# The first FFN of a decoder trunk, from eight block products to seven

## The chip, the core and the metric

One core of a Trainium2 chip runs the whole program in one launch. The metric is the time of one execution on the device in microseconds (us); the core has a matrix engine (PE, with a part PEld that loads weights), a vector engine (DVE), an activation engine (ACT), a general engine (POOL), and a queue engine (SP) that here only issues transfers. POOL issues transfers too, those that add to what lies in their target.

## What is computed

A trunk of two layers on one sequence of 512 tokens, model width 1024, all in float32. Each layer is: a half-step SwiGLU FFN (hidden width 2816), a token mixer, and another half-step FFN. The mixer of the first layer is a short gated convolution, that of the second a sparse attention. So there are six sub-layers, here numbered s = 0 to 5: FFN, convolution, FFN, FFN, attention, FFN. Each of them does

```python
h = rms_norm(x, g) * (1 + scale) + shift          # adaLN
x = x + HALF * gate * ((silu(h @ w_g) * (h @ w_u)) @ w_out)   # an FFN
```

with shift, scale and gate (1024 numbers each) from the conditioning vector c: `mod = silu(c) @ ada_w + ada_b`. That is a product of one row with a 1024 x 18432 matrix for the two layers: each of its 144 pieces of 128 outputs is done on DVE, as a row sum over a 128 x 1024 tile that is read from memory (512 KB), not on PE. The text calls such a piece a **modulation tile**; sub-layer s has 24 of them (8 scale, 8 shift, 8 gate).

## The kernel before

The state x lies in SBUF as eight tiles of 128 channels x 512 tokens. Every float32 product is made of three products of rounded parts (`mm3`, L167 to L170): high by high, high by low, low by high, so each operand is kept as a high part and a low part. A weight tile comes in by `weights` (L172): SP issues the load into `wraw`, ACT copies it to `whi`, DVE subtracts to get `wlo` (`split`, L163). `wraw`, `whi` and `wlo` have three buffers each in the pool `wp`.

**The usual FFN** (`ffn`, L462; s = 2, 3 and 5). The 22 hidden blocks j of 128 columns each need a gate product g and an up product u. The first two j are done plainly while the normalised input is still coming (`head_start`, L342, tile `hs`), the third as a `pair` (L407), each half of the tokens for itself; a plain j is 2 x 8 x 3 = 48 products of 512 columns, or twice as many of 256. Then `quarters` (L314) forms four sums of the quarters of h (tiles `th`, `tl`), and the remaining 19 j go by `seven_products` (L471): the 2 x 2 block product that makes g and u for two halves of the depth and two halves of the tokens takes seven block products of 4 x 3 matmuls each at 256 columns, so 84, and sums of weight quarters beside it. For these SP loads two quarters into the tile `qa`, POOL issues a transfer that adds a third quarter to both (L488), SP loads the whole block into `wraw` and a quarter into `a22`; DVE adds (L492, L493) and everything is split into high and low parts. `qa` has four places in turn: two of a pool `swa`, and two (`hhi1`, `hlo1`) that the second token half of h leaves when the third j is done (L477 to L479). The sums of the products are DVE's (L521 to L527). The output product runs in four parts of the hidden blocks (`FOUR` = 6, 6, 6, 4): after a part, for each of eight output blocks d, one weight tile, 3 x 6 matmuls of 512 columns into `y`, and an addition to x on DVE (L557). The last part goes in token halves, so that the next norm can begin.

**The first FFN** (`ffn_first`, L419; s = 0) is another function: all 22 j plain, three of them in its head (L433), with the modulation tiles of s = 0 between them (`ada_first`, L142); three output parts of 8, 7 and 7. It loads weights through further buffers of the pool `ap` (argument `own`), which also has four buffers for modulation tiles.

**The order of the modulation tiles.** They are jobs in a list (`todo`, L1192); `spread` (L370) hands a few to each step of a stage. The code gives the first FFN the 16 of its head, 8 gate tiles, all 24 of s = 1 and 12 of s = 2; the convolution (`conv`, L595) gets the other 84. A framework orders the instructions of every engine when the kernel is built, by their place in the program and by when operands and buffers are free, so a job may run earlier than its place. At run time each engine, SP's queue too, works in its built order. A small table for the attention's bias (`bias_table`, L649, eight matmul instructions in plain float32) is made in the first FFN by the job `small` (L1200).

PSUM has eight banks; six of them serve the products in turn (`psum`, L71), two the norm and the attention.

Of the kernel before, what the change touches and what calls it, by code (L numbers as in the profile page):

```python
# [12 lines left out]
F32 = mybir.dt.float32  # L13
# [15 lines left out]
PARTS = ((0, 8), (8, 15), (15, 22))  # L29
# [23 lines left out]
def decoder_kernel(ctx, tc, xT, cT, ng, adaw, adab, ffi, ffo, cwi, cw, cwo,  # L53
# [30 lines left out]
    ap = ada_es.enter_context(tc.tile_pool(name="ada", bufs=4))  # L84
    cond = ap.tile([P, D], F32, name="cond", bufs=1)
    x = [cst.tile([P, T], F32, name=f"x{d}") for d in range(KD)]
    ngs = cst.tile([P, NSUB * KD], F32, name="ngs")
    adabs = cst.tile([P, NSUB * NMOD], F32, name="adabs")
    for d in range(KD):
        (nc.sync if d < KD - 2 else nc.gpsimd).dma_start(x[d], xT[d])  # L90
    nc.sync.dma_start(cond, bass.AP(tensor=cT.tensor, offset=cT.offset, ap=[[0, P], [1, D]]))
    nc.gpsimd.dma_start(ngs, ng)
    nc.gpsimd.dma_start(adabs, adab)
    one = ap.tile([P, 1], F32, name="one", bufs=1)
# [12 lines left out]
    nc.scalar.activation(cond, cond, AF.Silu)  # L107
# [7 lines left out]
    def ada_tile(ap, s, t):  # L115
        raw = ap.tile([P, D], F32, name="adaraw")
        nc.sync.dma_start(raw, adaw[s * NADA + t])
        m = mods[:, s * NMOD + t:s * NMOD + t + 1]
        nc.vector.tensor_tensor_reduce(out=raw, in0=raw, in1=cond, scale=1.0, scalar=0.0,  # L119
                                       op0=ALU.mult, op1=ALU.add, accum_out=m)  # L120
# [12 lines left out]
    def ada_gate(s):  # L133
        c = s * NMOD + 2 * KD
        if s % 3 == 1:
            nc.vector.tensor_add(mods[:, c:c + KD], mods[:, c:c + KD], adabs[:, c:c + KD])
        else:
            nc.vector.tensor_add(mods[:, c:c + KD], mods[:, c:c + KD], adabs[:, c:c + KD])
            nc.vector.tensor_scalar(mods[:, c:c + KD], mods[:, c:c + KD], 0.5, None, op0=ALU.mult)


    def ada_first(ap, d):  # L142
        n = 1 if d < 2 else 2
        if d % n == 0:
            for c in range(d, d + n):
                ada_tile(ap, 0, c)
                ada_tile(ap, 0, KD + c)
            ada_scale(0, d, d + n)
            ada_shift(0, d, d + n)

    def ada_jobs(ap, s):
        lo = 2 * KD if s == 0 else 0
        jobs = [(lambda t=t: ada_tile(ap, s, t)) for t in range(lo, NADA)]

        def end():
            if s:
                ada_scale(s, 0, KD)
                ada_shift(s, 0, KD)
            ada_gate(s)
        return jobs + [end]  # L160
# [22 lines left out]

    def project(o, w, wc, h, ks, first, last, a=0, b=T):
        c = slice(wc * P, (wc + 1) * P)
        for n, (kw, k) in enumerate(ks):
            mm3(o, w[0][:, kw, c], w[1][:, kw, c], h[0][k][:, a:b], h[1][k][:, a:b],
                first and n == 0, last and n == len(ks) - 1)
# [29 lines left out]
    class Norm:  # L218
# [62 lines left out]
        def whole(self, d):  # L281
            sc, sh = mod(self.s, 0, d), mod(self.s, 1, d)
            xr = tmp("xr")
            nc.vector.scalar_tensor_tensor(xr, x[d], sc, self.all, op0=ALU.mult, op1=ALU.mult)
            nc.scalar.activation(self.hi[d], xr, AF.Identity, bias=sh)
            nc.vector.scalar_tensor_tensor(self.lo[d], xr, sh, self.hi[d], op0=ALU.add, op1=ALU.subtract)
# [8 lines left out]
        def alloc_seven(self, hp, tf, tt):  # L295
# [6 lines left out]
            self.th = [tt.tile([P, KD // 2, HT], F32R, name=f"th{j}") for j in range(4)]  # L302
            self.tl = [tt.tile([P, KD // 2, HT], F32R, name=f"tl{j}") for j in range(4)]
# [10 lines left out]
        def quarters(self):  # L314
# [92 lines left out]
    def pair(f, j, h, own=None, halves=False):  # L407
        gu = []
        for c in range(2):
            w = ffn_in(f, j, c, own if c else None)  # L410
            o = psum("gu")
            for a, b in HALVES if halves else ((0, T),):
                project(o[:, a:b], w, 0, h, [(k, k) for k in range(KD)], True, True, a, b)
# [5 lines left out]
    def ffn_first(s, f, nrm, nxt, extra, ahead, first, soon, own):  # L419
        with ExitStack() as es:  # L420
            hp = pool(es, "hp", 1)
            hid = Hidden(es, 18)
            h = nrm.alloc(hp)
            nj = FIRST
            early = spread(soon, PARTS[0][1] - nj)
            late = spread(extra, NJ - PARTS[0][1] + 2 * KD)

            def fill():
                early() if soon else late()

            js = [(j, c) for j in range(nj) for c in range(2)]
            w, os = [], [psum("hs") for _ in js]
            for d in range(KD):  # L433
                first(d)
                if d < len(js):
                    w.append(ffn_in(f, *js[d], own=own if d > 2 else None))
                nrm.whole(d)
                for n in range(len(w)):
                    for k in range(0 if n == d else d, d + 1):
                        project(os[n], w[n], 0, h, [(k, k)], k == 0, k == KD - 1)  # L440
            for j in range(nj):
                hid.activate(os[2 * j], os[2 * j + 1])
            for p, (j0, j1) in enumerate(PARTS):
                for j in range(max(j0, nj), j1):
                    hid.activate(*pair(f, j, h, own))
                    fill()
                n = j1 - j0
                a, ka = (hid.hi[j0:j1], hid.lo[j0:j1]), [(k, k) for k in range(n)]
                last = p == len(PARTS) - 1
                for d in range(KD - 3 if last else KD):  # L450
                    w = ffn_out(f, d, 1, j0, j1, own if d % 2 else None)
                    o = psum("y")
                    project(o, w, 0, a, ka, True, True)
                    if last:
                        residual(s, d, o, nxt)
                    else:
                        fill()
                        nc.vector.scalar_tensor_tensor(x[d], o, mod(s, 2, d), x[d], op0=ALU.mult, op1=ALU.add)
            assert not extra
            return tail(s, nxt, [(d, ffn_out(f, d, 1, j0, j1, own), 0, ka) for d in range(KD - 3, KD)], a, ahead)  # L460

    def ffn(s, f, nrm, nxt, w0, ahead):  # L462
        with ExitStack() as es:
# [3 lines left out]
            nj = 2  # L467
# [3 lines left out]
            def seven_products(j):  # L471
# [60 lines left out]
            swa = pool(es, "swa", 1, side="right")  # L532
            with ExitStack() as tf_es:
                nrm.alloc_seven(hp, pool(tf_es, "tf", 1), tt)
                h = nrm.hi, nrm.lo
                with ExitStack() as hw_es:
                    hw = pool(hw_es, "hw", 1)
                    w = w0 + [weights(ffi[f, j, c], KD, P, hw, 1, wp) for j, c in js[len(w0):]]
                    os = head_start(nrm, h, [(lambda k, w=w_: (w, 0, k)) for w_ in w])
# [7 lines left out]
            for p, (j0, j1) in enumerate(FOUR):  # L547
                for j in range(max(j0, nj), j1):
                    seven_products(j)
                n = j1 - j0  # L550
                a = (hid.hi[j0:j1], hid.lo[j0:j1])
                if p < len(FOUR) - 1:
                    for d in range(KD):
                        w = ffn_out(f, d, 1, j0, j1)
                        o = psum("y")
                        project(o, w, 0, a, [(k, k) for k in range(n)], True, True)
                        nc.vector.scalar_tensor_tensor(x[d], o, mod(s, 2, d), x[d], op0=ALU.mult, op1=ALU.add)  # L557
            sw_es.close()
# [3 lines left out]
            for i, d in enumerate(range(0, KD, 2)):  # L562
                if i < 2:
                    ws.append(ffn_out(f, d, 2, j0, j1))
                else:
                    t = (2, 0)[i - 2]
                    to = [tt.tile([P, KD // 2, HT], F32R, name=f"t{e}{t}").rearrange("p a b -> p (a b)") for e in "hl"]
                    raw = swa.tile([P, 2, KD * P // 2], F32, name="qa", bufs=2).rearrange("p a b -> p (a b)")
# [26 lines left out]
    def conv(s, nrm, nxt, extra, w0, ahead, own):  # L595
        with ExitStack() as es:
            h_es = es.enter_context(ExitStack())
# [594 lines left out]
    todo = [j for s in range(NSUB) for j in ada_jobs(ap, s)]  # L1192
# [7 lines left out]
    def small():  # L1200
# [5 lines left out]
        bias_table()  # L1206

    def ffn_ahead(f):
# [3 lines left out]
    soon = upto(1)  # L1212
# [5 lines left out]
    nrm, nxt = nxt, Norm(3)  # L1218
    w = ffn(2, 1, nrm, nxt, w, ffn_ahead(2))
# [80 lines left out]
```

## Time and profile before

| what | value |
|---|---|
| median of 3 runs | 2034.22 us (2033.07 to 2038.92) |
| the profiled execution | 2035.68 us |
| its span in the trace | 2033.9 us, 32445 instructions |
| mean granted PE clock | 0.988 of full speed |
| PE busy | 1962.4 us (96%) |
| DVE busy | 1494.8 us (73%) |
| ACT busy | 875.3 us (43%) |
| POOL busy | 202.1 us (10%) |
| moved by DMA | 307.39 MB, mean 151 GB/s |

The span runs from the first instruction to the last; 1.8 us of the profiled execution lie around it. In a row of a window, "(x868)" is the count of instructions, "PEclk" the granted clock of PE as a share of full speed, and the DMA share is the mean busy share of the 16 DMA engines. In a row of waits stand who waited for whom, the us in total, how often, and the longest. Matmuls overlap, so what one costs is read from how many fit into a stretch, not from its own length.

### The profile page before, as it was taken

How to read it: one execution, taken by the hardware profiler on the slowest of the kernel's cores; microseconds unless marked ns; L12 is line 12 of the kernel's file. 1: busy time of each engine (PE TensorE's matmuls, PEld its weight loads, DVE VectorE, ACT ScalarE, POOL GpSimd, SP SyncE). 2: the span in 40 equal slices, each digit the busy share in tenths (PEclk: the TensorE clock that was granted, in tenths of full speed). 3: DMA queues.
4: the chain of work that ended last, by engine and by line, in shares of the span. 5: the costliest groups of instructions: out<-in, count | busy, mean ns of one | idle time of the engine just before them, and what ended most of it. 6: DMA issues, size and time to landing. Idle time of an engine off the chain costs nothing.

```text
span 2033.9 us, 32445 instructions
## 1 busy us (share of the span) xinstructions
PE 1962.4 (96%) x12644; PEld 1766.0 (87%) x12644; DVE 1494.8 (73%) x2597; ACT 875.3 (43%) x1410; POOL 202.1 (10%) x279
## 2 busy tenths in 40 slices
PE   5999999999998999999999999999999898999999
PEld 3878888888897898999989899999888788898989
DVE  7888888664467586768768676886887886686865
ACT  3322222332244343434534343455777755343532
POOL 0000000100011000000100000002354520000000
PEclk9999999999998999999999999999999999999999
DMA  8889988322237464533646453133111125565621
GB/s 303 301 311 320 333 317 323 141 97 83 83 84 199 123 171 137 153 114 84 184 137 172 137 153 113 45 137 104 53 51 49 58 63 142 145 169 146 167 78 63
DMA packets 113046, 307.39 MB, mean 151 GB/s; under 512 B 13883, under 2 KB 14155, under 8 KB 112892
## 3 DMA queue, kind: packets, MB, share of 16 engines
q1 hardware_dynamic: 97164, 274.81, 39.2%
q0 software_dynamic: 15728, 30.51, 8.6%
q8 instruction: 99, 1.62, 0.3%
q14 instruction: 55, 0.45, 0.1%
HBM read 302.12 MB, written 3.15 MB: 150 GB/s over the span
## 4 chain that ended last, share of the span: by engine, by line
PE 83%; DVE 8%; ACT 4%; DMA 2%; issue 2%; SPq 0%; POOL 0%; ACTq 0%; DVEq 0%; POOLq 0%
PE gu L168 13%; PE gu L169 13%; PE gu L170 13%; PE y L168 7%; PE y L169 7%; PE y L170 7%; PE cv L169 2%; PE cv L168 2%; PE hs L168 2%; PE hs L169 2%; PE cv L170 2%; PE hs L170 2%; DVE wlo L165 1%; PE ty L169 1%; PE ty L168 1%
## 5 line engine op out<-in xcount | busy, mean ns | idle before, releaser
L164 ACT ACTIVATE whi<-wraw 128x1024 fp32r<-128x1024 f32 (+2 forms) x286 | 285.3, 1001 | 552.0 <-PE y L169 262.8
L165 DVE TENSOR_TENSOR wlo<-wraw,whi 128x1024 fp32r<-128x1024 f32 (+2 forms) x286 | 330.0, 1157 | 65.2 <-ACT whi L164 62.1
L168 PE MATMUL gu<-hhi,whi 128*128 128x256 f32 (+1 forms) x856 | 273.8, 320 | 4.3 <-ACT whi L164 4.2
L169 PE MATMUL gu<-hlo,whi 128*128 128x256 f32 (+1 forms) x856 | 273.8, 320 | 0.0
L170 PE MATMUL gu<-hhi,wlo 128*128 128x256 f32 (+1 forms) x856 | 272.0, 318 | 0.2 <-DVE wlo L165 0.2
L168 PE MATMUL y<-ahi,whi 128*128 128x512 f32 x587 | 230.6, 395 | 0.2 <-ACT ahi L164 0.2
L170 PE MATMUL y<-ahi,wlo 128*128 128x512 f32 x587 | 230.7, 396 | 0.0
L169 PE MATMUL y<-alo,whi 128*128 128x512 f32 x587 | 230.4, 395 | 0.0
L119 DVE CUSTOM_DVE_ANT_0 adaraw<-adaraw,cond 128x1024 f32<-128x1024 f32 x144 | 173.4, 1222 | 21.1 <-DMA adaraw<-in_adaw 20.0
L168 PEld LDWEIGHTS gu<-hhi,whi 128*128 128x128 f32 x856 | 161.5, 189 | 19.8 <-ACT whi L164 5.6
L169 PEld LDWEIGHTS gu<-hlo,whi 128*128 128x128 f32 x856 | 161.4, 189 | 13.1
L170 PEld LDWEIGHTS gu<-hhi,wlo 128*128 128x128 f32 x856 | 160.8, 188 | 13.7 <-DVE wlo L165 0.6
L488 POOL DMA_DIRECT2D qa<-in_ffi x57 | 68.6, 1204 | 838.2 <-DVE qal L165 240.1
L168 PE MATMUL gu<-th,qah 128*128 128x256 f32 x456 | 130.1, 285 | 12.3 <-ACT p L515 12.3
L168 PEld LDWEIGHTS y<-ahi,whi 128*128 128x128 f32 x587 | 109.5, 188 | 29.2 <-ACT ahi L164 3.3
L169 PEld LDWEIGHTS y<-alo,whi 128*128 128x128 f32 x587 | 110.2, 188 | 27.9 <-DVE alo L165 1.8
L170 PEld LDWEIGHTS y<-ahi,wlo 128*128 128x128 f32 x587 | 110.2, 188 | 25.6
L557 DVE SCALAR_TENSOR_TENSOR x<-y,mods,x 128x512 f32<-128x512 f32 x72 | 54.0, 750 | 106.2 <-PE y L170 106.2
L168 PE MATMUL gu<-th,qbh 128*128 128x256 f32 x456 | 128.2, 281 | 2.4 <-ACT qbh L164 2.4
L169 PE MATMUL gu<-tl,qah 128*128 128x256 f32 x456 | 129.5, 284 | 0.0
L170 PE MATMUL gu<-th,qbl 128*128 128x256 f32 x456 | 128.4, 282 | 0.7 <-DVE qbl L165 0.7
L170 PE MATMUL gu<-th,qal 128*128 128x256 f32 x456 | 129.0, 283 | 0.0
(295 smaller groups left out, 5146.9 us busy)
## 6 DMA issues: line engine op xcount, KB each, us to landing
adaraw<-in_adaw SPq DMA_DIRECT2D x144, 512.0 KB, 5.6
wraw<-in_ffi SPq DMA_DIRECT2D x119, 512.0 KB, 3.7
qa<-in_ffi SPq DMA_DIRECT2D x114, 256.0 KB, 3.9
qa<-in_ffi POOLq DMA_DIRECT2D x57, 512.0 KB, 5.7
wraw<-in_ffo SPq DMA_DIRECT2D x72, 384.0 KB, 3.8
a<-in_ffi SPq DMA_DIRECT2D x57, 256.0 KB, 3.6
wraw<-in_cwi SPq DMA_DIRECT2D x24, 512.0 KB, 3.3
wraw<-in_nwi SPq DMA_DIRECT2D x20, 512.0 KB, 3.4
```

The lines of the kernel that those rows point to most:

```text
L119: nc.vector.tensor_tensor_reduce(out=raw, in0=raw, in1=cond, scale=1.0, scalar=0.0, op0=ALU.mult, op1=ALU.add, accum_out=m)
L164: nc.scalar.activation(hi, src, AF.Copy)
L165: nc.vector.tensor_tensor(lo, src, hi, ALU.subtract)
L168: nc.tensor.matmul(o, sh, mh, start=first, stop=False)
L169: nc.tensor.matmul(o, sh, ml, start=False, stop=False)
L170: nc.tensor.matmul(o, sl, mh, start=False, stop=last)
L488: nc.gpsimd.dma_start(qa, bass.AP(tensor=a21.tensor, offset=a21.offset, ap=[a21.ap[0], [0, 2], a21.ap[1]]), accum_op=ALU.add)
L557: nc.vector.scalar_tensor_tensor(x[d], o, mod(s, 2, d), x[d], op0=ALU.mult, op1=ALU.add)
```

## The change

`ffn_first` is gone; `ffn` does s = 0 too (it is called without first weights, and then has three plain j in its head and one as a `pair`, so 18 of the 22 j go by seven products). Its head is that of `ffn_first`, with h in the layout of the others: the first half of the depth lies in two token halves, so `project` and `whole` take it in pieces of 256 tokens. `pair` no longer runs one token half after the other, but both within each step of the depth.

The extra weight buffers of `ap` are gone in the first FFN. In its head, modulation tiles have three buffers of a pool `hw` and two that later hold `th1` and `tl1`; three of the six head weights are split into places of `tt`. After the head, in the first FFN and in the FFN of s = 2, a modulation tile takes one of the three `wraw` buffers. In these two FFNs `qa` has three places in turn in place of four (one of `swa`). The convolution has a pool of its own with four buffers.

The modulation tiles are handed out anew: the first FFN keeps its 60 (two jobs' fills after each of j = 4 and 5, one or two in each output step, one per later j), the convolution gets 60 and `bias_table`, the FFN of s = 2 the last 24 (those of s = 5).

The start: c comes as one row of 4 KB by POOL's queue, PE spreads it over the partitions with two float32 matmuls, and ACT takes SiLU from PSUM; before, a transfer of 512 KB brought it to all partitions. All eight x tiles come by SP's queue; two came by POOL's.

The core of the diff:

```diff
-    cond = ap.tile([P, D], F32, name="cond", bufs=1)
+    crow = wp.tile([P, D], F32, name="wraw", tag="wraw", bufs=3)[0:1]
+    nc.gpsimd.dma_start(crow, cT)
...
+    for c in range(D // T):
+        o = psum("cb", "nat")
+        nc.tensor.matmul(o, ones[0:1], crow[:, c * T:(c + 1) * T], start=True, stop=True)
+        nc.scalar.activation(cond[:, c * T:(c + 1) * T], o, AF.Silu)
...
     def project(o, w, wc, h, ks, first, last, a=0, b=T):
         c = slice(wc * P, (wc + 1) * P)
-        for n, (kw, k) in enumerate(ks):
...
+        todo = [(kw, k, p) for kw, k in ks
+                for p in (HALVES if b - a > HT and isinstance(h[0][k], Halves) else ((a, b),))]
...
-    def ffn(s, f, nrm, nxt, w0, ahead):
+    def ffn(s, f, nrm, nxt, w0, ahead, soon=(), extra=()):
...
-            nj = 2
+            nj = 2 if w0 else FIRST
+            modulated = bool(soon or extra)
...
-                i = (j - nj) % 4
-                qa = (swa.tile([P, 2, QT], F32, name="qa", bufs=2) if i < 2 else
-                      hp.tile([P, 2, QT], F32, name="qa", tag=("hhi1", "hlo1")[i - 2]))
+                qa = next(sums)()
...
+            n = 1 if modulated else 2
+            sums = cycle([sum_tile(swa, bufs=n)] * n + [sum_tile(hp, tag=t) for t in ("hhi1", "hlo1")])
...
+                        rows = cycle([(hw, "adaraw", 3)] * 3 + [(tt, "th1", 1), (tt, "tl1", 1)])
...
-                os += pair(f, nj, h, halves=True)
-                nrm.quarters()
+                if modulated:
+                    ada_raw[0] = lambda: wp.tile([P, D], F32, name="wraw", tag="wraw", bufs=3)
+                os += pair(f, nj, h)
+                nrm.quarters(tt)
             nj += 1
+            early = spread(soon, 2 * (FOUR[0][1] - nj) + KD // 2)
+            late = spread(extra, NJ - FOUR[0][1] + 2 * (len(FOUR) - 1) * KD - (KD if soon else 0))
...
                 for j in range(max(j0, nj), j1):
                     seven_products(j)
+                    if p or soon:
+                        fill(1 if p else 2)
...
                         w = ffn_out(f, d, 1, j0, j1)
+                        fill(1 if soon else 2)
...
-    w = ffn_first(0, 0, nrm, nxt, [small] + upto(2, NADA // 2), lambda: [weights(cwi[c], KD, P) for c in range(3)],
-                  lambda d: ada_first(ap, d), soon, ap)
+    w = ffn(0, 0, nrm, nxt, None, lambda: [weights(cwi[c], KD, P) for c in range(3)], upto(1), [small] + upto(2, NADA // 2))
     nrm, nxt = nxt, Norm(2)
-    w = conv(1, nrm, nxt, upto(6), w, ffn_ahead(1), ap)
+    w = conv(1, nrm, nxt, [bias_table] + upto(5), w, ffn_ahead(1))
+    nrm, nxt = nxt, Norm(3)
+    w = ffn(2, 1, nrm, nxt, w, ffn_ahead(2), extra=upto(6))
```

More of the change, by code (lines that the diff above doesn't have):

```diff
@@ L28 @@
 NJ = FF // P
-PARTS = ((0, 8), (8, 15), (15, 22))
 FOUR = ((0, 6), (6, 12), (12, 18), (18, 22))
@@ L405, in activate, with pair @@
             self.keep(af)
-    def pair(f, j, h, own=None, halves=False):
+    def pair(f, j, h):
         gu = []
         for c in range(2):
-            w = ffn_in(f, j, c, own if c else None)
+            w = ffn_in(f, j, c)
             o = psum("gu")
-            for a, b in HALVES if halves else ((0, T),):
-                project(o[:, a:b], w, 0, h, [(k, k) for k in range(KD)], True, True, a, b)
+            project(o, w, 0, h, [(k, k) for k in range(KD)], True, True)
             gu.append(o)
@@ L415, in pair @@
         return gu
[L419 to L460, printed above, removed]
@@ L592, in ffn, with conv @@
             return nxt_w
-    def conv(s, nrm, nxt, extra, w0, ahead, own):
+    def conv(s, nrm, nxt, extra, w0, ahead):
         with ExitStack() as es:
+            own = pool(es, "cw", 1)
+            ada_raw[0] = lambda: own.tile([P, D], F32, name="adaraw", bufs=4)
             h_es = es.enter_context(ExitStack())
@@ L1191, in decoder_kernel @@
     nrm.start()
-    todo = [j for s in range(NSUB) for j in ada_jobs(ap, s)]
+    todo = [j for s in range(NSUB) for j in ada_jobs(s)]
     def upto(s, n=0):
```

102 lines of the change are left out of this document (61 added, 41 removed).

## The prediction

> **What bounds the kernel now.** I read the page first: how busy PE is, and what the chain that ended last is made of.
>
> ```profile
> span 2033.9 us, 32445 instructions
> PE 1962.4 (96%) x12644; PEld 1766.0 (87%) x12644; DVE 1494.8 (73%) x2597; ACT 875.3 (43%) x1410; POOL 202.1 (10%) x279
> PE 83%; DVE 8%; ACT 4%; DMA 2%; issue 2%; SPq 0%; POOL 0%; ACTq 0%; DVEq 0%; POOLq 0%
> ```
>
> PE is busy 96% of the span and makes 83% of the chain. So a matmul taken away is time taken away, if what feeds PE still keeps up. The windows by stage come next. I cut them where the first product of each sub-layer starts: first FFN, convolution, FFN of s = 2, of s = 3, and of s = 5.
>
> ```profile
> 25.00:405.00 380.00, 375.95 (x1661) 304.24 (x1661) 311.78 (x498) 110.45 (x139) 6.31 (x4) 1.00 0.82 295
> 405.00:584.00 179.00, 178.57 (x923) 151.36 (x922) 93.10 (x163) 52.88 (x73) 7.02 (x4) 1.00 0.26 89
> 584.00:941.00 357.00, 347.62 (x2489) 325.31 (x2488) 258.94 (x374) 152.60 (x212) 25.28 (x21) 0.99 0.51 143
> 941.00:1297.00 356.00, 351.74 (x2521) 329.03 (x2520) 264.06 (x391) 155.20 (x217) 24.04 (x19) 0.99 0.47 134
> 1666.00:2034.00 368.00, 355.60 (x2565) 332.90 (x2565) 258.15 (x369) 147.75 (x203) 20.60 (x18) 0.99 0.46 129
> ```
>
> The columns are the stretch, its length, then busy time and count of PE, PEld, DVE, ACT and POOL, PEclk, DMA share and GB/s. The first FFN takes 380 us where two with seven products take 356 and 357; the last one's 368 holds the output's end as well. PE idles 4 us in the first FFN, 9.4 and 4.3 in those two: seven products cost idle time that the plain form doesn't have. The modulation tiles stand in their own windows (DVE busy and count of these instructions alone).
>
> ```profile
> L119 DVE CUSTOM_DVE_ANT_0 adaraw<-adaraw,cond 128x1024 f32<-128x1024 f32 x144 | 173.4, 1222 | 21.1 <-DMA adaraw<-in_adaw 20.0
> 0.00:400.00 400.00, 173.44 (x144) 1.00 0.82 296
> 405.00:584.00 179.00, 0.00 (x0) 1.00 0.26 89
> ```
>
> All 144 ran before 400 us, though the code hands 84 of them to the convolution: the built order pulled them forward as their four buffers allowed. That is why DMA is at 295 GB/s in the first FFN and at 89 in the convolution.
>
> **The change part by part.** *The products.* PE's pace is read from stretches in which it never waits: plain ones of 512 columns, then seven products of 256.
>
> ```profile
> 150.00:350.00 200.00, 200.00 (x868) 162.48 (x867) 171.29 (x265) 51.75 (x62) 0.00 (x0) 1.00 0.90 322
> 700.00:750.00 50.00, 50.00 (x431) 50.00 (x430) 41.94 (x56) 24.85 (x34) 4.81 (x4) 1.00 0.59 162
> ```
>
> 200 us / 868 = 0.2304 us for 512 columns, 50 us / 431 = 0.1160 us for 256. A plain j costs 48 x 0.2304 = 11.06 us, one by seven products 84 x 0.1160 = 9.74 us. For 18 j: 18 x (11.06 - 9.74) = **23.7 us saved**. The four plain j now run half of their depth in 256 columns: 192 x 0.1160 - 96 x 0.2304 = 0.2 us more. The output products keep their columns.
>
> The Trainium skill has a formula for this pace (TensorE: Matmul & The Clock Gate, section Back-to-back issue gap): N / 2.4 + 2.5 ns for one isolated matmul of N columns at full clock, 109.2 ns for 256 and 215.8 for 512. By it, an estimate, the 18 j would save 21.4 us; the rows above show both paces some 6% slower, and the measured paces decide.
>
> *The entry into seven products.* What PE waited for in the first FFN, then in those of s = 2, 3 and 5 (its larger waits only):
>
> ```profile
> PE hs L168 <- ACT hhi L285: 3.5, 2, 2.0
> PE hs L170 <- DVE wlo L165: 1.8, 2, 0.9
> ```
> ```profile
> PE gu L168 <- ACT p L515: 4.5, 1, 4.5
> PE gu L168 <- ACT whi L164: 3.3, 2, 3.2
> PE gu L168 <- ACT qbh L164: 1.1, 1, 1.1
> ```
> ```profile
> PE gu L168 <- ACT qbh L164: 1.3, 1, 1.3
> PE gu L168 <- ACT p L515: 0.8, 1, 0.8
> ```
> ```profile
> PE gu L168 <- ACT p L515: 7.0, 1, 7.0
> ```
>
> Seven products begin with 8.9, 2.1 and 7.0 us of waiting, on average 6.0. ACT's timeline at the first of them says for what:
>
> ```profile
> 643.76 1.06 ACT L164 ACTIVATE qah<-qa 128x1024 fp32r<-128x1024 f32 x1 [9.46 <-DMA qa<-in_ffi]
> 644.72 0.61 ACT L164 ACTIVATE qbh<-a 128x512 fp32r<-128x512 f32 x1
> ```
>
> ACT stood 9.46 us before a split of a `qa` whose accumulating transfer was late, and what PE needed (`qbh` from `a22`, then the copy `p`) was queued behind it. That was the third seven-product j, the first to load into a place left by the plain h. In the new first FFN the second one already does so, since `swa` has one place. A wait has a second price:
>
> ```profile
> 646.60:651.70 5.10, 5.10 (x24) 5.10 (x25) 5.10 (x8) 1.31 (x2) 0.00 (x0) 0.50 0.43 121
> ```
>
> After the 4.5 us wait the granted clock was 0.50 for 5.1 us, 24 matmuls where 44 fit: 2.3 us lost. The Trainium skill (TensorE: Matmul & The Clock Gate, section What's actually happening) gives this as a gate that falls to half speed after an idle window of about 3.4 us and opens after as long a busy one; the trace agrees (0.50), and its 5.1 us is what I use. I take 6.0 + 2.3, rounded to **8.5 us**, for the new entry; the ends are 2.1 (s = 3) and 8.9 + 2 x 2.3 = 13.5 (s = 2). The four sums of `quarters` and their splits come before it on ACT and DVE; they hide beside the 11 us of the fourth j.
>
> *Rows in DVE's way.* In the first FFN, 44 tiles follow the head. Each `seven_products` gets 38 jobs / 56 fills = 0.68 of one, each output step twice that, 1.36. DVE works 41.94 of 50 us in the pure seven-product stretch, 8.2 of 9.74 us for a j; with 0.68 x 1.22 it is 9.0, under PE's 9.74. An output step lasts 18 x 0.2304 = 4.15 us:
>
> ```profile
> L165 DVE TENSOR_TENSOR wlo<-wraw,whi 128x768 fp32r<-128x768 f32 (+1 forms) x7 | 7.2, 1029 | 0.3 <-ACT whi L164 0.3
> L557 DVE SCALAR_TENSOR_TENSOR x<-y,mods,x 128x512 f32<-128x512 f32 x72 | 54.0, 750 | 106.2 <-PE y L170 106.2
> ```
>
> DVE then has 1.03 + 0.75 + 1.36 x 1.22 = 3.4 us in 4.15. DMA has 384 KB + 1.36 x 512 KB in 4.15 us, 266 GB/s by the 1024-byte KB, under the 322 at which PE ran freely above. So neither is full, and the queue of buffers (first rival) is what can bite: **2 us**, with 0 and that rival's 28 as ends.
>
> *The convolution* gets 60 tiles, 73 us of DVE, and `bias_table`, whose eight matmuls only move, from the first FFN to here, as the chain of waits shows them:
>
> ```profile
> 127.81 3.63 PE pt L663 x8
> ```
>
> 93.1 + 73 = 166 of 179 us is full but no more, and its DMA was at 89 GB/s. If the order pulls rows forward as before, they lie beside its input products:
>
> ```profile
> 450.00:550.00 100.00, 100.00 (x434) 81.24 (x433) 45.13 (x59) 25.45 (x30) 0.00 (x0) 1.00 0.24 84
> ```
>
> There DVE is free 55 us of 100. If not, its five output steps of 24 x 0.2304 = 5.5 us each get 4.6 tiles, 5.6 us of DVE beside 2 of their own: 2.1 x 5 = 10 us. I take **2 us**, ends 0 and 10.
>
> *The FFN of s = 2* gets 24 tiles (29 us of DVE beside 258.94 of 357) and loses a `qa` place: its second j will wait where its third did. The interleaved `pair` frees `hhi1` a quarter pair, 2.8 us, sooner. **1 us**, from -4 to 7. In s = 3 and 5 only this earlier freeing is new: **-1 us**, -3 to 2.
>
> *The start.* DVE's chain of norm and rows sets PE's first product:
>
> ```profile
> 13.33 1.04 ACT L107 ACTIVATE cond<-cond 128x1024 f32<-128x1024 f32 x1
> 16.63 1.23 DVE L119 CUSTOM_DVE_ANT_0 adaraw<-adaraw,cond 128x1024 f32<-128x1024 f32 x1
> 25.47 0.79 PE L168 MATMUL hs<-hhi,whi 128*128 128x512 f32 x1 [2.01 <-ACT hhi L285]
> ```
>
> A row of 4 KB and two PE products should give `cond` before 13.3 us, so that a row or two run while DVE waits for PE's norm; against it stand all x on one queue and the low parts in halves. **-1 us**, -4 to 3.
>
> Sum: -23.7 + 0.2 + 8.5 + 2 + 2 + 1 - 1 - 1 = **-12.0 us**. From the profiled execution's 2035.68 us (its span 2033.9 and 1.8 around it) that is 2023.7; the median of the runs, 2034.22, lies 1.5 lower, so **2022.2 us**.
>
> **The rivals.** *Slower: three `wraw` buffers are too few in the output steps.* Weights and rows now share them, and SP's queue stands still at the first load without a buffer, with the weights of the next step behind it. A buffer is held from issue to its last reader:
>
> ```profile
> adaraw<-in_adaw SPq DMA_DIRECT2D x144, 512.0 KB, 5.6
> wraw<-in_ffo SPq DMA_DIRECT2D x72, 384.0 KB, 3.8
> ```
>
> A row holds it 5.6 + 0.4 issue + 1.2 = 7.2 us, a weight 3.8 + 0.4 + 0.9 + 1.0 = 6.1. For 2.36 of them a step takes (1.36 x 7.2 + 6.1) / 3 = 5.3 us, not 4.15: 24 steps x 1.15 = 28 us, and 2022 + 26 = 2048 us. Against it: 5.6 us was measured at 295 GB/s, and three weights split ahead give each of the three parts up to 8 us of lead, enough for 8 x 1.15 = 9 us nearly. It makes the kernel slower when the lead is gone and the price passes 18 us, a mean hold above 6.2 us. Chance 0.21.
>
> *No change: the new waits eat the gain.* The entry at its 13.5, the convolution at 10, s = 2 at 5: 2022.2 + 5 + 8 + 4 = 2039 at the most; half of it gives 2031. For it: six head sums fill all six PSUM banks, and the fourth j needs two back, behind `quarters` on ACT. Chance 0.15.
>
> *More gain: the entry as in s = 3 (2.1 us), the rows hidden, the start 1 us better:* 2022.2 - 6.4 - 4 - 1 = 2011 us. Chance 0.19.
>
> *The change doesn't do what it says:* the order moves the rows elsewhere, as it did before. Rows have no buffers of their own in the two FFNs, so they can't run far ahead; if s = 2 had none of its 24, the time would still be near 2022. Chance 0.02.
>
> **How the numbers follow.** A measurement here tells 0.3% (6.1 us) from no change, so faster is below 2028.1 and slower above 2040.3. The forecast has 0.43 with its own range 2015 to 2028, more gain 0.19, rows moved elsewhere 0.02, no change 0.15, slower 0.21. The first three are faster: 0.64; same 0.15, slower 0.21. The range runs from 2009, past the better case, to 2043, into the slower one, and leaves out about 0.17 above and 0.03 below.
>
> **What would show it.** The first FFN's stage should shrink from 380 us to about 363 (-23.5, +8.5 + 2, and the table's 3.6 gone), with PE's waits before the second seven-product j of 4 to 9 us and a clock of 0.5 behind them; `y` matmuls every 0.2304 us in its output steps (one every 0.29 is the first rival); no row in the last 24 later than the stage of s = 2; the convolution should come to 179 + 3.6 + 2 = 185 us. A first FFN over 380 us, or rows waiting for a DMA while PE waits for `wlo` of an output weight, would make the prediction wrong.

## The result and the profile after

The changed kernel takes **2090.22 us** (median of 4 runs, 2089.32 to 2092.19) where the kernel before took 2035.57 on the same chip: a ratio of 1.0269, 95% interval 1.0251 to 1.0287. It is slower by 54.7 us. The forecast was 2022.2, the range 2009 to 2043, the chance of slower 0.21. The profiled execution took 2089.32 us with a span of 2087.2.

First the page: the span, the busy times, and what the chain that ended last is made of.

```profile
span 2087.2 us, 34348 instructions
PE 1991.0 (95%) x13353; PEld 1823.9 (87%) x13353; DVE 1594.3 (76%) x2780; ACT 919.5 (44%) x1490; POOL 216.2 (10%) x292
PE 72%; DVE 12%; DMA 6%; ACT 4%; issue 3%; SPq 1%; POOL 0%; DVEq 0%; ACTq 0%; POOLq 0%
```

PE's part of the chain fell from 83% to 72%; DVE's rose from 8% to 12%, DMA's from 2% to 6%. PE now stands still for others in places. The windows by stage follow, cut where the first product of each sub-layer starts: first FFN, convolution, FFN of s = 2 and of s = 3, first of before at these cuts, then of after.

```profile
25.47:405.50 380.03, 376.15 (x1662) 304.24 (x1662) 311.81 (x499) 110.48 (x139) 6.31 (x4) 1.00 0.82 295
405.50:587.20 181.70, 181.57 (x949) 154.56 (x950) 95.81 (x170) 54.30 (x77) 7.02 (x4) 1.00 0.26 87
587.20:950.00 362.80, 352.18 (x2522) 329.49 (x2520) 264.22 (x388) 154.17 (x216) 25.28 (x21) 0.99 0.51 143
950.00:1305.65 355.65, 351.87 (x2521) 329.17 (x2521) 263.69 (x390) 155.22 (x218) 24.04 (x19) 0.99 0.47 135
```
```profile
20.95:430.00 409.05, 374.34 (x2435) 341.45 (x2435) 333.58 (x532) 153.45 (x215) 21.68 (x18) 0.96 0.71 214
430.00:618.70 188.70, 188.58 (x952) 157.69 (x953) 149.37 (x268) 55.48 (x79) 7.06 (x4) 0.98 0.63 221
618.70:998.20 379.50, 363.07 (x2499) 338.30 (x2497) 289.91 (x441) 153.25 (x216) 25.32 (x21) 0.97 0.61 170
998.20:1358.80 360.60, 355.49 (x2496) 331.77 (x2496) 263.99 (x390) 155.47 (x218) 24.04 (x19) 1.00 0.48 133
```

Against before the start is 4.5 us earlier, the first FFN 29.0 longer, the convolution 7.0, the FFN of s = 2 16.7 and that of s = 3 5.0; what follows takes as long as before (728.4 and 728.3). That is the span's +53.3. (In what follows PE is busy 5.1 us longer and waits 5.0 us less.) Two rows want two explanations. In the first FFN PE is idle 409.05 - 374.34 = 34.7 us, where it was idle 3.9. In the FFN of s = 3, which has no row sums and whose loops the diff leaves almost alone, PE is idle about as long as before (5.1 and 3.8 us) and yet the stage grew by 5 us.

What PE waited for in the first FFN after, the larger waits only:

```profile
PE y L173 <- ACT ahi L169: 10.8, 4, 3.8
PE pr L266 <- DVE dg L265: 6.1, 1, 6.1
PE gu L175 <- DVE wlo L170: 4.9, 1, 4.9
PE pr L258 <- DVE nacc L241: 4.7, 1, 4.7
```

The first line has no counterpart in before's first FFN. It lies at the **seams**: a run of seven-product j ends, the last j's hidden tile is made on DVE and ACT, and the first output step `y` needs it. Here is one seam in the timelines of after, PE (the last product of the j, then the first `y` that needs its hidden tile), ACT, and DVE.

```profile
208.15 0.28 PE L175 MATMUL gu<-hhi,qbl 128*128 128x256 f32 x1
216.93 1.22 PE L173 MATMUL y<-ahi,whi 128*128 128x512 f32 x2 [2.91 <-ACT ahi L169]
```
```profile
214.87 0.63 ACT L492 ACTIVATE e<-e 128x512 f32<-128x512 f32 x1 [5.83 <-DVE e L491]
216.25 0.63 ACT L169 ACTIVATE ahi<-e 128x512 fp32r<-128x512 f32 x1 [0.76 <-DVE e L493]
```
```profile
207.46 1.22 DVE L125 CUSTOM_DVE_ANT_0 wraw<-wraw,cond 128x1024 f32<-128x1024 f32 x1
...
210.34 0.69 DVE L487 TENSOR_TENSOR e<-gu,p 128x512 f32<-128x512 f32 x1
211.28 1.23 DVE L125 CUSTOM_DVE_ANT_0 wraw<-wraw,cond 128x1024 f32<-128x1024 f32 x1 [0.25 <-DMA wraw<-in_adaw]
...
212.43 0.42 DVE L488 TENSOR_TENSOR e<-gu,e 128x256 f32<-128x256 f32 x1
...
215.53 0.69 DVE L493 SCALAR_TENSOR_TENSOR e<-e 128x512 f32<-128x512 f32 x1 [0.76 <-ACT e L492]
216.14 1.22 DVE L125 CUSTOM_DVE_ANT_0 wraw<-wraw,cond 128x1024 f32<-128x1024 f32 x1
217.28 0.69 DVE L170 TENSOR_TENSOR alo<-e,ahi 128x512 fp32r<-128x512 f32 x1
```

PE's last product ends at 208.4, and `ahi` is there at 216.9. Row sums (L125) stand in that chain three times: one at 207.46, ahead of the last j's first step (L487 at 210.34); one at 211.28, between L487 and L488, which also waited 0.25 us for its own load with the chain queued behind it; one at 216.14, ahead of `alo`. Each is 1.22 us. PE had `y` products of the earlier k to run meanwhile, and still stood 2.91 us. The windows around it show the second price:

```profile
212.00:217.00 5.00, 2.09 (x10) 1.38 (x8) 4.21 (x8) 1.26 (x2) 0.00 (x0) 0.93 0.48 157
217.00:222.00 5.00, 5.00 (x12) 3.98 (x13) 2.58 (x5) 0.84 (x1) 0.00 (x0) 0.50 0.29 105
```

The granted clock was 0.50 from 217 to 222: 12 matmuls in 5 us, where 21.7 of 0.23 us fit. The Trainium skill (TensorE: Matmul & The Clock Gate, section What's actually happening) halves the clock after an idle window of about 3.4 us; the trace agrees with the 0.50, but here 2.9 us of idle time were enough. Shorter waits of after went either way: in the 5 us from 805.3, behind a wait of 1.9 us, the mean granted clock was 0.66, and in the 5 us from 903.0, behind one of 2.3 us, it was 1.00.

The first FFN's end shows the same on another chain. DVE's timeline at the norm there:

```profile
423.47 0.15 DVE L211 TENSOR_TENSOR rs_b<-rs_a,nv 128x2 f32<-128x2 f32 x1
423.54 1.22 DVE L125 CUSTOM_DVE_ANT_0 adaraw<-adaraw,cond 128x1024 f32<-128x1024 f32 x1
...
424.76 0.15 DVE L212 SCALAR_TENSOR_TENSOR rs_r<-rs_b,rs_r 128x2 f32<-128x2 f32 x1
```

Between steps of 0.15 us, each waiting for the one before it, stand rows of 1.22 us, four of them from 420.96 to the first `dg` at 426.04. They are the convolution's rows, which have buffers of their own and so can run this early. 6.1 us for `dg` and 4.7 for `nacc` stand among PE's waits.

The s = 3 surprise is a pace. Windows in its seven products with PE busy throughout and the clock at 1.00, before and after:

```profile
1060.00:1110.00 50.00, 50.00 (x432) 50.00 (x432) 43.84 (x59) 25.46 (x36) 4.85 (x4) 1.00 0.58 156
```
```profile
1110.00:1160.00 50.00, 50.00 (x420) 50.00 (x419) 42.64 (x59) 25.53 (x35) 4.81 (x4) 1.00 0.62 162
```

432 matmuls became 420, 0.1157 us became 0.1190, with the same instructions and the same tiles. What differs is where the tiles lie: the change moved the [P, 1] scratch column `one`, which only one early activation uses, from the pool `ap` to `sp`, and the pools opened later (h, split weights) begin 32 bytes further on.

### The profile page after: what moved, and what is told of

It reads as the page before. It is cut to its first block, busy times and chain, and to the rows that moved or that the text cites. A ratio compares the mean times of both kernels' runs of the same rounds, so it can differ in the third digit from the quotient of the medians.

```text
span 2087.2 us, 34348 instructions
## 1 busy us (share of the span) xinstructions
PE 1991.0 (95%) x13353; PEld 1823.9 (87%) x13353; DVE 1594.3 (76%) x2780; ACT 919.5 (44%) x1490; POOL 216.2 (10%) x292
## 4 chain that ended last, share of the span: by engine, by line
PE 72%; DVE 12%; DMA 6%; ACT 4%; issue 3%; SPq 1%; POOL 0%; DVEq 0%; ACTq 0%; POOLq 0%
PE gu L173 10%; PE gu L175 10%; PE gu L174 10%; PE y L173 7%; PE y L174 7%; PE y L175 7%; DMA qa<-in_ffi 3%; DMA wraw<-in_adaw 2%; PE cv L173 2%; PE cv L174 2%; PE cv L175 2%; PE ty L174 2%; PE ty L173 2%; PE ty L175 2%; PE hs L174 2%
## 5 line engine op out<-in xcount | busy, mean ns | idle before, releaser
L169 ACT ACTIVATE whi<-wraw 128x1024 fp32r<-128x1024 f32 (+1 forms) x267 | 261.0, 981 | 439.3 <-PE y L174 226.8
L170 DVE TENSOR_TENSOR wlo<-wraw,whi 128x1024 fp32r<-128x1024 f32 (+1 forms) x267 | 301.5, 1132 | 57.1 <-ACT whi L169 55.4
L173 PE MATMUL y<-ahi,whi 128*128 128x512 f32 x576 | 230.4, 403 | 18.1 <-ACT ahi L169 18.1
L173 PE MATMUL gu<-hhi,whi 128*128 128x256 f32 (+1 forms) x696 | 203.2, 292 | 4.4 <-ACT whi L169 4.4
L175 PE MATMUL gu<-hhi,wlo 128*128 128x256 f32 (+1 forms) x696 | 201.9, 291 | 5.0 <-DVE wlo L170 4.9
L174 PE MATMUL gu<-hlo,whi 128*128 128x256 f32 (+1 forms) x696 | 201.1, 289 | 0.0
L173 PE MATMUL gu<-th,qah 128*128 128x256 f32 x600 | 173.4, 289 | 11.6 <-ACT p L481 11.6
L175 PE MATMUL gu<-th,qbl 128*128 128x256 f32 x600 | 171.8, 286 | 2.4 <-DVE qbl L170 2.2
L174 PE MATMUL gu<-tl,qah 128*128 128x256 f32 x600 | 172.4, 287 | 0.0
L175 PE MATMUL gu<-th,qal 128*128 128x256 f32 x600 | 172.3, 287 | 0.0
L174 PE MATMUL gu<-tl,qbh 128*128 128x256 f32 x600 | 170.4, 284 | 0.0
```

Source lines behind the costliest of these rows:

```text
L169: nc.scalar.activation(hi, src, AF.Copy)
L170: nc.vector.tensor_tensor(lo, src, hi, ALU.subtract)
L173: nc.tensor.matmul(o, sh, mh, start=first, stop=False)
L174: nc.tensor.matmul(o, sh, ml, start=False, stop=False)
L175: nc.tensor.matmul(o, sl, mh, start=False, stop=last)
```

## The experiments

Four causes stood against each other: **order** (row sums in the chains that end a run of seven products and the first FFN's norm), **ring** (three `wraw` buffers are too few, the prediction's first rival), **place** (the 32 bytes), and the **products** themselves (seven for eight does not pay). All ratios are to the kernel before, which took 2032.8 to 2037.1 us on the chips used; after stands at 1.0269. Each ratio has an interval of 4 to 6 us to either side, so a difference of two runs is known to some 6 us. Of each edit the core is shown.

**a_align** undoes the 32 bytes alone, in the changed kernel:

```diff
-    one = sp.tile([P, 1], F32, name="one", bufs=1)
...
-    rowm = cst.tile([P, 1], F32, name="rowm")
+    rowm = one = cst.tile([P, 1], F32, name="rowm")
```

> The kernel after, with one scratch column taken out, so that every tile allocated behind it lies 32 bytes lower, at an address that 64 divides as in the kernel before; the order of the work is the same. Theory of the place: 256-column matmuls of seven products go from 0.1193 us back to 0.1160, 75 blocks x 84 x 0.0033 = 21 us less than after. Rival, that DMA or DVE traffic slows PE's reads: no change, within 2 us of after.

**b_shift** makes them alone, in the kernel before:

```diff
-    one = ap.tile([P, 1], F32, name="one", bufs=1)
+    one = sp.tile([P, 1], F32, name="one", bufs=1)
```

> The kernel before, with the same scratch column moved so that the tiles of the seven-product FFNs lie 32 bytes higher. Theory of the place: 57 blocks x 84 x 0.0033 = 16 us more than before, pace 0.119 in the FFNs of s = 2, 3 and 5. Rival: no change, within 2 us of before.

a_align: 2075.39 us, 1.0205 [1.0188, 1.0222], 0.64% or 13 us better than after. b_shift: 2054.3 us, 1.0107 [1.0086, 1.0127], 20 us worse than before with one column of scratch moved. The same pace windows, of a_align in s = 3 and of b_shift in s = 5:

```profile
1100.00:1150.00 50.00, 50.00 (x432) 50.00 (x432) 42.25 (x57) 25.25 (x35) 4.81 (x4) 1.00 0.62 163
```
```profile
1800.00:1850.00 50.00, 50.00 (x420) 50.00 (x419) 42.63 (x59) 25.52 (x35) 4.81 (x4) 1.00 0.60 157
```

432 and 420 in 50 us: the pace goes with the place, whichever kernel it is. At 0.0033 us a matmul, the 57 j by seven products of before (84 matmuls each) come to 16 us, the 75 of after to 21; measured were 20 for b_shift and 13 for a_align, so this sum gives the order of the size and not the size. In s = 5 of after, whose total hid it, a run of six j with its output part takes 94.2 us where it took 92.5 before.

**d_norow** leaves out the 68 modulation tiles behind the first FFN's head and in the FFN of s = 2, loads and sums:

```diff
     def ada_tile(s, t):
+        if left_out[0]:
+            return
         raw = ada_raw[0]()
```

> The kernel after without the 44 modulation tiles behind the first FFN's head and the 24 of the FFN of s = 2: neither loaded nor summed, their modulations are left out (zero). Theory of the seams (row sums in DVE's queue delay the chain that ends a run of seven products): the waits of y for ahi, 18 us in after, go, and with them some 14 us of half clock, so 30 us less than after. Rival, that the seven products by themselves are slow at their entry: less than 12 us.

**c_nosum** keeps their loads and leaves out the sums:

```diff
         nc.sync.dma_start(raw, adaw[s * NADA + t])
+        if left_out[0]:
+            return
```

> The kernel after, in which the 68 modulation tiles of the first FFN (behind its head) and of the FFN of s = 2 are still loaded into the shared buffers but not summed on DVE; their modulations are left out (zero). Theory of the seams (the sums on DVE cost the time): 34 to 38 us less than after, as without the tiles at all. Rival, the one of the prediction (three shared buffers and the loads behind them): at most 10 us less than after, and y matmuls slower than 0.2304 us in output steps.

d_norow: 2053.75 us, 1.0098 [1.0080, 1.0116], so these rows cost 1.71% or 35 us. Its first FFN and that of s = 2 take 383.5 and 368.0 us, where after's took 409.05 and 379.5, and no wait of `y` for `ahi` is left. c_nosum: 2067.12 us, 1.0153 [1.0125, 1.0181]: without the sums 24 of the 35 us are gone, which lies between the two expectations. What is left, 11 us, belongs to the loads, and here they cost once and not at every step. PE's longest wait, and what ACT did before it:

```profile
PE y L177 <- ACT ahi L173: 11.9, 1, 11.9
115.27 1.06 ACT L173 ACTIVATE qah<-qa 128x1024 fp32r<-128x1024 f32 x1 [12.34 <-DMA qa<-in_ffi]
```

This one wait lies at the first output part. ACT stood 12.34 us for a late transfer into `qa`, with the hidden tile's steps queued behind it: the wait that the prediction had found at the entry. The two later output parts take 33.8 us, 4.23 for each of eight steps, as in d_norow. A ring too small would have held up every step. After itself has no such wait of 11.9 us (its first output part waits 2.3 and 1.8), so the 24 and 11 us are not the shares of sums and loads in after.

**e_convlate** lets the convolution's rows and bias table go only after the last piece of the first FFN's norm:

```diff
-                fill()
+                with tc.issue_after(nrm.done):
+                    fill()
```

> The kernel after with the convolution's row sums queued on DVE behind the last piece of its norm. Theory of the norm's chain (row sums fill every gap between its short DVE steps): the 13 us of PE's waits at the end of the first FFN fall to about 4, with the half clock behind them 12 to 16 us less than after; the convolution itself, with DVE at 80%, may give 0 to 5 back. Rival, that the FFN's last part is slow for its own sake: no change.

2078.16 us, 1.0217 [1.0194, 1.0241]: 0.52% or 11 us better than after, a little less than expected. The end of the first FFN, the same piece of work in after and here:

```profile
391.25:430.00 38.75, 25.83 (x205) 24.82 (x203) 33.64 (x88) 12.89 (x25) 0.00 (x0) 0.84 0.71 246
```
```profile
388.80:419.40 30.60, 25.73 (x204) 24.58 (x202) 23.81 (x67) 13.20 (x25) 0.00 (x0) 0.94 0.55 195
```

38.75 us became 30.6, with PE's busy time unchanged. DVE lost 9.8 us of busy time there, eight rows. PE's waits for `dg` and `nacc` fell to 1.3 and 2.5 us.

**f_seam** keeps all rows and moves them out of the seams: none behind the last two j of a run, four together at the first FFN's first j by seven products, and those of an output part only after the run's last `alo` (`hid.done`):

```diff
-                    if p or soon:
-                        fill(1 if p else 2)
+                    if p and j + 2 < j1:
+                        fill(1)
+                    elif soon and j == nj:
+                        fill(4)
...
-                        fill(1 if soon else 2)
+                        with tc.issue_after(hid.done):
+                            fill(1 if soon else 2)
```

> The kernel after with the row sums kept off the end of each run of seven products: none is handed out after the last two j of a part, and those of the output steps are queued on DVE behind the last j's low part. Theory of the seams: the waits of y for ahi fall from 18 us to under 4, and the time by 20 to 30 us. Rival, that it is the amount of DVE work and not its place: less than 8 us.

2077.11 us, 1.0197 [1.0177, 1.0216]: 0.72% or 15 us of the 35, between the two expectations. The seams are clean (1.6 us of `y` for `ahi`, where after had 18.1), but waits have moved to the starts of runs. PE's two lines, and ACT before the longest new one:

```profile
PE gu L173 <- ACT p L481: 18.0, 7, 4.3
PE gu L173 <- ACT whi L169: 9.6, 6, 4.0
157.02 1.06 ACT L169 ACTIVATE whi<-wraw 128x1024 fp32r<-128x1024 f32 x1 [7.08 <-DMA wraw<-in_ffi]
```

After had 11.6 and 4.4 us in these two lines. Not all of the first is the rows' doing: d_norow, without the 68 rows, has 17.7 us there, all at its four entries into seven products. New in f_seam are 4.3, 2.1 and 1.4 us early in the three later runs of the first FFN. Each time ACT had just stood for a weight load into `wraw` (7.1, 2.1 and 2.8 us), whose buffers and queue the weights share with the rows.

**h_th** is a_align with 32 bytes more on the other side of the memory, so that the tiles of `th` move too:

```diff
+    pad = pool(ctx, "pad", 1, side="right").tile([P, 1], F32, name="pad")
```

> a_align with one scratch column more at the far end of SBUF, so that the tiles th and tl (the moving operand of five of the seven products) lie at multiples of 64 bytes too. If the moving operand's address counts as the weights' does, those 60 of 84 matmuls go from 0.1170 to 0.1138 us: 75 x 60 x 0.0032 = 14 us less than a_align. If only the weights' address counts: as a_align, within 2 us.

2077.35 us, 1.0189 [1.0167, 1.0211], which is a_align's 1.0205 within the intervals. That is the second expectation's time, but not its reason. By the trace, from start to start, `y` matmuls went from 233.5 ns to 229.1, and those of `th` with the sum `qa` from 117.2 to 119.9: one gain, one loss.

**g_all** joins a_align, e_convlate and f_seam, edit for edit.

> The kernel after with three edits together: the addresses of a_align, the convolution's rows behind its norm, the FFNs' rows off the ends of the runs. If the three causes add, 15 + 12 + 25 = 52 us less than after, 2038 us, within 8. If they hide one another, 2050 or more.

2051.05 us, 1.0063 [1.0043, 1.0083]: 42 us better than after, about the sum of the three as measured (13 + 11 + 15 = 39). So the causes add within the intervals; the expectation came out too low because it counted 25 us for f_seam. 13 us over before are left.

**j_place** runs nothing but runs of 96 matmuls, no other part of the computation, with weights and moving columns at byte offsets 0, 32, 64 and 96 (mod 128):

```diff
+                    nc.tensor.matmul(o[:, 0:n], W[r % 3 == 2][:, wo + c * P:wo + (c + 1) * P],
+                                     M[r % 3 == 1][:, mo + k * n:mo + (k + 1) * n], start=r == 0, stop=r == N - 1)
```

> Nothing of the trunk: only runs of 96 matmuls on PE, each with its own weight load, 256 or 512 columns, with the weights at 0, 32, 64 or 96 bytes and the moving operand at 0, 32, 64 or 96 bytes behind a multiple of 128, and nothing else in SBUF's traffic but one copy out of PSUM a run. If the address alone sets the pace: 256 columns at 0.114 to 0.117 us with the weights at a multiple of 64 and 0.120 with them at 32 or 96. If the address only matters together with the other engines' traffic: all sixteen pairs within 0.001 us.

It was executed once, at a mean granted clock of 0.999. A copy on DVE ends each run, so the difference of two copies' starts is the time of 96 matmuls. First 256 columns with weights at 64 and moving columns at 0, 32, 64, 96, behind the copy of the run before; then the same for 512 columns with weights at 32:

```profile
109.67 0.42 DVE L74 COPY raw<-n256w32m 128x256 f32<-128x256 f32 x1 [10.88 <-PE n256w32m L72]
120.56 0.42 DVE L74 COPY raw<-n256w64m 128x256 f32<-128x256 f32 x1 [10.47 <-PE n256w64m L72]
131.92 0.42 DVE L74 COPY raw<-n256w64m 128x256 f32<-128x256 f32 x1 [10.93 <-PE n256w64m L72]
143.43 0.42 DVE L74 COPY raw<-n256w64m 128x256 f32<-128x256 f32 x1 [11.09 <-PE n256w64m L72]
154.74 0.42 DVE L74 COPY raw<-n256w64m 128x256 f32<-128x256 f32 x1 [10.89 <-PE n256w64m L72]
...
288.92 0.69 DVE L74 COPY raw<-n512w0m 128x512 f32<-128x512 f32 x1 [21.72 <-PE n512w0m L72]
311.31 0.69 DVE L74 COPY raw<-n512w32m 128x512 f32<-128x512 f32 x1 [21.70 <-PE n512w32m L72]
333.08 0.69 DVE L74 COPY raw<-n512w32m 128x512 f32<-128x512 f32 x1 [21.07 <-PE n512w32m L72]
355.48 0.69 DVE L74 COPY raw<-n512w32m 128x512 f32<-128x512 f32 x1 [21.71 <-PE n512w32m L72]
377.46 0.69 DVE L74 COPY raw<-n512w32m 128x512 f32<-128x512 f32 x1 [21.29 <-PE n512w32m L72]
```

At 256 columns: 10.89, 11.36, 11.51 and 11.31 us, or 113.4, 118.3, 119.9 and 117.8 ns each; equal places (64 and 64) are the slowest, 64 and 0 the fastest. At 512 columns: 22.39, 21.77, 22.40 and 21.98 us, or 233.2, 226.8, 233.3 and 229.0 ns; there equal places are the fastest. Places 32, 64 and 96 paired with themselves give the same as here. So neither expectation holds: with nothing else running the place sets the pace, but as a pair, and a pair is good or bad by the width of the moving columns.

This fits the 32 bytes. As the programs are built, the split sums `qah` and `qbh` (weights) lie at 64 in before and `th` (moving columns) at 96; in after both lie at 96. j_place gives 117.8 and 119.8 ns for these two pairs, and the traces of before and after show 117 and 120 ns from start to start for `th` with the sums. In h_th both lie at 64, again an equal pair.

**k_closure** puts the products to the test: d_norow with a_align and e_convlate, so seven for eight in the first FFN without the rows in its way (the 68 tiles are left out as in d_norow).

> The kernel after with the addresses of a_align, the convolution's rows behind its norm, and without the 68 modulation tiles of the two FFNs (left out, zero). If addresses, norm chain and rows are the whole of the loss, 15 + 12 + 36 = 63 us less than after: 2027 us, below the kernel before, with the first FFN's stage at 370 us or less. If something else of the new first FFN costs time too: 2035 or more.

2023.58 us, 0.9937 [0.9917, 0.9957]. Its profiled execution, at 2013.82, lies 10 us below that median, mostly behind s = 3, so only its first FFN and FFN of s = 3 are read here:

```profile
22.50:392.00 369.50, 357.10 (x2435) 329.36 (x2435) 277.91 (x414) 156.96 (x215) 21.68 (x18) 0.99 0.56 164
939.40:1294.80 355.40, 349.54 (x2497) 326.07 (x2497) 263.48 (x390) 155.12 (x218) 24.04 (x19) 1.00 0.48 135
```

The first FFN takes 369.5 us, 10.5 less than before, and s = 3 takes what it took before. The time is the first expectation's; a kernel before without these 68 tiles was not run, but before's first FFN has only 3.9 us of idle PE that it could win by that.

**i_spread** is g_all with the rows handed out more thinly: some of them go on to the FFN of s = 3.

```diff
-    ..., upto(1), [small] + upto(2, NADA // 2))
+    ..., upto(1), [small] + upto(2))
-    w = conv(1, nrm, nxt, [bias_table] + upto(5), w, ffn_ahead(1))
+    w = conv(1, nrm, nxt, [bias_table] + upto(4), w, ffn_ahead(1))
-    w = ffn(2, 1, nrm, nxt, w, ffn_ahead(2), extra=upto(6))
+    w = ffn(2, 1, nrm, nxt, w, ffn_ahead(2), extra=upto(5))
-    w = ffn(3, 2, nrm, nxt, w, lambda: nsa_in(4))
+    w = ffn(3, 2, nrm, nxt, w, lambda: nsa_in(4), extra=upto(6))
```

> g_all with the rows handed out more evenly: 32 in the first FFN behind its head, 48 in the convolution, 24 in each of the FFNs of s = 2 and 3. If it is the count of rows on DVE in the first FFN that still costs there: 8 to 12 us less than g_all, 2040 us. If what is left there is the entry and the start of each run: as g_all, within 3 us.

2037.87 us, 1.0009 [0.9989, 1.0029]: level with before, and 0.54% or 11 us better than g_all, as the first expectation had it. So the count of rows in the first FFN matters beside their place; its stage went from g_all's 400.1 us to 380.9. But all rows are computed now, and the gain of the products is gone: k_closure, which differs in the rows alone, was 14 us faster. Two lines of PE's waits hold most of that:

```profile
PE gu L172 <- ACT p L480: 18.9, 8, 7.5
PE gu L172 <- ACT whi L168: 11.4, 5, 6.6
```

These are 30 us of the seven products waiting for the copy `p` and for weights, where k_closure has 14.9 and 4.4 in the same lines, 11 us less. (Before, with three FFNs by seven products, had 12.3 and 4.2.) Whether they could be had back by another order was not tried.

**n_before_place** and **o_spread_place** change the places alone, in the kernel before and in i_spread: 96 bytes on the right side, and `poss` taken from them.

```diff
+    pad = pool(ctx, "pad", 1, side="right").tile([P, 24], F32, name="pad")
...
-            poss = cm.tile([P, 16], F32, name="poss")
+            poss = pad[:, 0:16]
```

> The kernel before with nothing changed but addresses: a pad of 96 bytes at the far end of SBUF (in which a small constant of the attention finds room) moves the tiles th, tl and the hidden activations to a multiple of 128 bytes. By the map of paces measured in j_place, weights at 64 with the moving operand at 0 take 0.1133 us for 256 columns, and equal places 0.2267 for 512: summed over the program's matmuls 24 us less than before, 2012 us, with th products near 0.113 and y products near 0.227 us. If the map holds only without other traffic: within 5 us of before.

> i_spread with the same pad. By the map 31 us less than i_spread, 2007 us, some 5 us below n_before_place. If seven products in the first FFN are worth nothing once the plain form runs at its best pace: as n_before_place or above.

n_before_place: 2024.52 us, 0.9959 [0.9938, 0.9981], the fastest whole kernel of this study. o_spread_place: 2032.63 us, 0.9997 [0.9977, 1.0016], no gain over i_spread that can be told, and 8 us slower than n_before_place. So with all rows computed, no order tried here made seven products in the first FFN pay. In n_before_place `y` went from 232.8 ns to 228.3 from start to start, the 256-column kinds stayed within 0.3 ns on average; 1761 x 4.5 ns = 7.9 us, about the 8 us measured. The gain is in the FFNs by seven products, where `y` went from 233.4 to 227.0 ns, j_place's time for equal places. The times of j_place had promised more than this to both: `th` with `qa` (64 and 0) runs at 117 ns in the kernels and not at 113.4. What else sets that pace stays open.

## Why the prediction was wrong

- **The products** (-23.7 us for 18 j): the mechanism is right. k_closure, without the 68 rows and with the old places, is 13 us faster than before, and its first FFN 10.5 shorter. The prediction had 380 -> 363 for this FFN with 2 us for rows, so 361 without; 8 us are missing. 4.9 of them are waits in the norm at its end (2.5 for `nacc`, 1.3 for `dg`, 1.1 for `hhi`); the rest was not taken apart.
- **The entry** (8.5 us, with 4 to 9 us of waiting before the second seven-product j): right, and for its reason. In after, the `pair` with the next two j takes 39.5 us where its matmuls make up 30.5 at before's paces and 31.2 at after's own, so 8 to 9 too much. The wait is 4.9 us, DVE had stood 6.9 us for a late `qa`, and the granted clock behind it was 0.50 for 5.4 us. In k_closure the wait is 5.1.
- **Rows in DVE's way** (2 us, ends 0 and 28): this is the step that failed. It added up DVE's busy time (3.4 of 4.15 us in an output step, 9.0 of 9.74 in a j) and found room. Room on average did not decide: a row sum stands in order on DVE between the links of a chain that PE waits for at each seam. Seven waits at six seams make 18.1 us in all, and behind the longest the granted clock was 0.50; the rows of the two FFNs cost 35 us by d_norow, and 24 us go with the sums alone by c_nosum. By f_seam 15 of the 35 go with the place at the seams; the rest was not taken apart. The FFN of s = 2, put at 1 us, has 11.5 of it (379.5 against 368.0).
- **The first rival** (three `wraw` buffers, 2048 us) ended on the right side largely by luck. Its sign would have been `y` every 0.29 us; in d_norow and in c_nosum's later parts a `y` step of 18 takes 4.23 us, 0.235 each, and in after `y` within a step keeps 0.2335. What it says of late loads is not empty: they make the wait of 11.9 us in c_nosum and those at the starts of runs in f_seam. How much of after's 35 us is theirs stays open.
- **The convolution** (2 us, ends 0 and 10): the cost was looked for inside it, beside its products. There it is small: 188.7 us, against 181.7 + 3.6 for the bias table + 2 = 187.3. But its rows ran ahead of it, into the first FFN's norm, and cost 11 us there by e_convlate (in that run the convolution itself takes 186.0). The prediction had seen that the built order pulls rows forward, and counted this as a help only.
- **Nothing for the places.** No step of the prediction looked at where a tile lies. The 32 bytes cost 13 us by a_align (21 by the pace), in all four FFNs. "In s = 3 and 5 -1 us" became +5 in s = 3.
- **The start** (-1 us): right in direction, 4.5 us in after, whose first product starts at 20.95, and 2.7 to 4.5 in the other runs with this start.

Rows 35, the convolution's rows 11 and places 13 make 59 of the 65 us between the forecast's -12 and the +53 of the span; k_closure, without all three, lies 3.32% or 68 us below after, which is their sum within the intervals.

## What to carry to other kernels

Filler work is not priced by the free time of its engine alone but by where the built order lets it stand: ask which short dependent chain the critical engine waits for, and how many fillers fit between its links. Hold fillers back from the end of such a chain by a dependency, and expect the wait to appear at the next start. After any change of allocations compare matmuls per 50 us in a stage that was not edited; if that moved, look at the addresses before looking at the schedule.

## What the runs showed of the hardware

The pace of a matmul depends on the byte places of its two operands, mod 128, and differently by width: from 113.4 to 120.0 ns at 256 columns, from 226.8 to 234.3 at 512, with nothing else running and the clock at 1.00, at the four places tried. The formula in the Trainium skill (TensorE: Matmul & The Clock Gate, section Back-to-back issue gap) gives 109.2 and 215.8 ns, and has no term for the place; j_place lies 4 to 10% above it. In a whole kernel such a place was worth 20 us, 1%, through a scratch column that no matmul reads.
